# Five tiles of u instead of ten take their low parts through DRAM, and ten pairs instead of eleven in the first half of the down projection

## The chip, the cores and the metric

The kernel runs on one core of one Trainium2 chip. The core has a matrix engine (TensorE, PE in the profile), a vector engine (VectorE, DVE), an activation engine (ScalarE, ACT), GpSimd (POOL) and SyncE (SP); each works through its own list of instructions in order and waits at an instruction until what it needs is there. Transfers between DRAM and the on-chip memory are issued by ACT, POOL and SP, each from its own list, and run on 16 DMA engines that all three share. The metric is the device time of one execution in microseconds, smaller is better; the median of three runs is given.

## The reference

One decoder layer on x of 256 tokens by 2048 columns, in float32: a pre-norm, one input projection, two kinds of attention, an output projection with a post-norm, and then the feed-forward part, which is where the change is:

```
x   = x + RMSNorm_post(concat_heads(A, B) @ W_out)
x   = x + RMSNorm_post2(W_down relu(RMSNorm_pre2(x) @ W_up)^2)
```

W_up is 2048 x 8192 and W_down 8192 x 2048. Below, u stands for relu(...)^2, 256 x 8192, that is 16 tiles of 512 columns, u0 to u15.

## The kernel before

**Products.** Every float32 operand x is split into a high part and a low part: ACT writes `hi` (L311, or L315 with a gain), which rounds x to TensorE's fp32r type, and DVE writes `lo` = x - `hi` (L312, L316). A product is three matmuls: hi by hi, hi by lo, lo by hi (L301), each of 128 rows by 512 columns. Weights come tile by tile: SP loads 512 KB `raw` (five buffers), ACT and DVE split them into `hi` and `lo` (eight buffers each), up to six tiles ahead of TensorE. TensorE has no other work that it could turn to when a `lo` is late.

**Pairs.** Two such k tiles can be taken together as a "pair", in a scheme with seven instead of eight products of blocks (function `seven`): 21 instead of 24 matmuls for both. For that, 1 MB of weights is loaded by POOL into one of the buffers `ab`, `ab2`, `c`, `ab_down`, `u01` (L379), DVE makes two sums t and u of it (L366 to L371), four parts are split instead of two, and DVE makes sums on the activations' side too (q, then s; L1035 to L1037). DOWN_SEVEN lists which pairs kp are taken so in the two halves of the down projection. The s of pairs that both halves take (SHARED) are written to DRAM in the first half (L1029) and read back by POOL in the second.

**The up projection** runs in eight chunks of 1024 columns of W_up, from 360 to 710 us. A chunk j gives u tiles 2j and 2j+1. Chunks from 1 on have plain k tiles and three pairs. When a chunk ends, DVE adds its partial sums (L1101, L1163), and four times (two u tiles by two token blocks) a chain follows while the next chunk runs: ACT makes r, relu and square (L944, L945), into the ring `r` of three buffers, and writes it to DRAM as `rkeep` in 512-byte pieces (L947); after D_BACK it issues the read back (`turn_u`, L956), which has to wait until the write has landed, into a quarter of buffer `c`; DVE transposes this into the tile `uT` (L965). The detour does the part of the transpose that crosses groups of 32 partitions.

**Low parts of u.** For the tiles g in AWAY, `lo_away` puts u - hi(u) together in DRAM during the up projection: ACT writes -hi(u) in two halves, `neg`, into the same ring `r` (L979), and sends each to DRAM (L981, `ukeep<-neg`); after D_ADD, POOL issues for each half a transfer that adds u to what is there (L991, an accumulate). In the first half of the down projection POOL reads this back as `ulo` (L1021). For the other tiles, DVE makes `ulo` there itself (L312), and SP writes it to `ukeep` for the second half (`keep_u`, L1025).

**The down projection** has two halves c of 1024 output columns. Each goes through the 16 tiles of u in order, tile g holding k = 4g to 4g+3, which are the pairs kp = 2g and 2g+1. In the first half, pairs' weights come into `ab_down` and `c` by turns.

**The end.** `x_back` brings x back for the residual: the powers `pwn` that it was scaled with, in four small reads (L1216), then sixteen reads of 128 KB from `xkeep` (L1221), all on SP, and DVE scales them (L1227). `powers`, which writes `pwk` (L859), runs during the output projection, near 326 us.

**What sets the order.** The program is written out in one go by a planner: `Flow` keeps a clock that advances with each matmul by a modelled time, and chains that are due at a moment of it. `flow.start(gen, delay)` puts a chain in, `yield d` lets it sleep for d. Whenever the clock passes a chain's moment, its next instructions are written into the engines' lists. So a delay such as D_BACK doesn't make an engine wait; it decides behind which other instructions on its list a step stands. Where a step stands before its input is there, the engine waits, with all that is listed behind it.

Of the kernel before, what the change touches and what calls it, by code (L numbers as in the profile page):

```python
# [18 lines left out]
F32 = mybir.dt.float32  # L19
# [7 lines left out]
P = 128  # L27
D = 2048
S = 256
NB = S // P  # L30
# [15 lines left out]
CW = 1024  # L46
# [46 lines left out]

UP_STEP = 2.4

D_BACK, D_TURN, D_NEG, D_LO, D_ADD = 8.0, 8.0, 9.0, 2.0, 25.0


SUMS_AHEAD = 2
# [17 lines left out]
N_SEVEN = [sum(w == "w" for w, _ in steps) for steps in UP_STEPS]  # L117


DOWN_SEVEN = ((7, 9, 11, 13, 15, 19, 21, 23, 25, 27, 29), range(3, 28, 2))  # L120
AWAY = range(4, 14)
LATE = 10
SHARED = [k for k in DOWN_SEVEN[0] if k in DOWN_SEVEN[1]]
GT = FF // 512
# [144 lines left out]
def layer(nc, tc, io):  # L269
    flow = Flow()  # L270
# [78 lines left out]
    late = {}  # L349
# [97 lines left out]
    for c in range(2):  # L447
        wide_d.append([])
        for what, k in DOWN_STEPS[c]:
            if what == "k":  # L450
                ts = [weights.plan(down_weight(c, k), 1, CW)]
            else:
                q, parts_q, back = [lambda c=c, k=k, f=f: f(c, k) for f in (down_sums, down_split, down_back)]
# [232 lines left out]
    for half in range(2):  # L686
        qkv = {}
        for nms in (("qk", "v") if not half else "qkv"):
            accs = [acc for _, _, acc in proj(xT, [ch_a[half, nms]], f"{nms}{half}",
                                              bank_of=at_bank if (half, nms) == (0, "v") else None)]  # L690
            for i, nm in enumerate(nms):
                t = pa.tile([P, NB, 512], F32, tag=nm, name=f"{nm}_{half}")
# [149 lines left out]
    pwk, pwn = dram.tile([P, NB], F32, name="pwk"), con.tile([P, NB], F32, name="pwn")  # L842
    xkeep = [dram.tile([P, D], F32, name=f"xkeep{b}") for b in range(NB)]

    def powers():
        po, g_post = late["po"], late["g_post"]
        yield 8.0
        for n in range(4):
            junk = po.tile([P, 512], BF16, tag="junk", bufs=1, name=f"junkg{n}")
            nc.scalar.activation(junk, g_post[:, n * 512:(n + 1) * 512], AF.Square, accum_out=gg4[:, n:n + 1])  # L850
            yield 1.5
        nc.vector.reduce_sum(gg, gg4, axis=mybir.AxisListType.X)
        nc.vector.tensor_scalar_add(pws[:, 3, :], ss0, gg)
        r = rstd_of(pws[:, 3, :], NB, D, "pw")
        yield 2.0
        nc.vector.tensor_single_scalar(out=pw.bitcast(I32), in_=r.bitcast(I32), scalar=0x7F800000, op=OP.bitwise_and)
        nc.vector.tensor_single_scalar(out=pwi.bitcast(I32), in_=pw.bitcast(I32), scalar=0x7F800000, op=OP.bitwise_xor)
        nc.vector.tensor_scalar_mul(pwi, pwi, 0.5)
        nc.gpsimd.dma_start(out=pwk, in_=pwi)  # L859
        for i, (v, c) in enumerate(((pwi, 1.0 / D), (pwi, EPS), (pw, EPS))):  # L860
            nc.vector.scalar_tensor_tensor(out=pws[:, i, :], in0=v, scalar=c, in1=v, op0=OP.mult, op1=OP.mult)
        for b in range(NB):
            for c in (slice(0, CW), slice(CW, D)):
                nc.vector.tensor_scalar_mul(xs[b][:, c], xs[b][:, c], pw[:, b:b + 1])
                yield 1.5
# [74 lines left out]
    def up_evac(j, b, acc, order):  # L940

        yield UP_STEP * order
        r = late["up"].tile([P, 512], F32, tag="r", bufs=3, name=f"r{j}_{b}")
        nc.scalar.activation(r, acc, AF.Relu, scale=rstd2[b])  # L944
        nc.scalar.activation(r, r, AF.Square)  # L945
        keep = dram.tile([P, 512], F32, name=f"rkeep{j}_{b}")
        nc.scalar.dma_start(out=keep.rearrange("(a t) (q c) -> (t q) a c", a=4, q=4),  # L947
                            in_=r.rearrange("m (a c) -> m a c", a=4))
        flow.start(turn_u(j, b, keep), D_BACK)

    turned = set()

    def turn_u(j, b, keep):

        x = closing()[2 * b + j % 2]
        nc.scalar.dma_start(out=x, in_=keep)  # L956
        yield D_TURN
        if j not in uT:
            if j in (0, 1, 10, 11, 12, 13):
                t2 = late["u01" if j < 2 else "ab2" if j < 12 else "ab"][:, j % 2 * CW:(j % 2 + 1) * CW]  # L960
            else:
                tag = {"tag": "T", "bufs": 2} if j > 13 else {"tag": f"uT{j}", "bufs": 1}
                t2 = late["up"].tile([P, CW], F32, name=f"uT{j}", **tag)
            uT[j] = t2.rearrange("p (k s) -> p k s", k=4)
        nc.vector.transpose(uT[j][:, :, b * P:(b + 1) * P].rearrange("p k (q t) -> p k q t", q=4),  # L965
                            x.rearrange("p (q k c) -> p k q c", q=4, k=4))
        if b:
            turned.add(j)
            if j in AWAY:
                flow.start(lo_away(j), D_NEG)  # L970
# [133 lines left out]
    def closing():  # L1104
        return [late["c"][:, i * 512:(i + 1) * 512] for i in range(4)]
# [62 lines left out]
    up = late["up"]  # L1168
# [40 lines left out]

    def x_back():  # L1210

        def in_order(rows):
            return rows.rearrange("(t q) d -> q t d", q=4)

        for q in range(4):
            nc.sync.dma_start(out=pwn[32 * q:32 * q + 32], in_=in_order(pwk)[q])  # L1216
        for b in range(NB):
            for i in range(2):
                x = uT[6 + 2 * b + i].rearrange("p k s -> p (k s)")
                for q in range(4):  # L1220
                    nc.sync.dma_start(out=x[32 * q:32 * q + 32], in_=in_order(xkeep[b])[q, :, i * CW:(i + 1) * CW])  # L1221
                yield 2.0
        yield 20.0
        for b in range(NB):
            for i in range(2):
                x = uT[6 + 2 * b + i].rearrange("p k s -> p (k s)")
                nc.vector.tensor_scalar_mul(x, x, pwn[:, b:b + 1])  # L1227
                yield 1.5
# [152 lines left out]
```

## Time and profile before

| | us |
|---|---|
| median of 3 runs | 1062.83 (1059.89, 1062.83, 1066.42) |
| profiled execution | 1065.99 |
| its span | 1064.2, granted TensorE clock 0.990 on average |
| TensorE busy | 1038.5 |
| VectorE busy | 833.6 |
| ScalarE busy | 639.2 |
| GpSimd busy | 74.4 |

A span that TensorE fills to 98% has little waiting in it, and what there is lies in a few places; so the busy shares say only which engine is the bound. Where time is lost is read from windows of 10 us: the number of matmuls in one, and the granted clock. Who is to blame is read from the timeline of the engine that was late, where each row has the idle time before the instruction and what ended it. For a transfer the time from issue to landing counts, not that of its issue.

### The profile page before, as it was taken

To read this page: it belongs to the slowest core of one execution; us is meant where nothing else is said; L and a number is where in the kernel's file an instruction comes from. 1 tells how busy PE (TensorE), PEld (TensorE's weight loads), DVE (VectorE), ACT (ScalarE), POOL (GpSimd) and SP (SyncE) were. 2 spreads that over 40 slices of the span, in tenths; PEclk is the share of its full clock that TensorE was granted. 3 is DMA by queue.
4 is the path that set the end of the run, shared out by engine and by line. 5 is a ranking of instruction groups with operands and counts; after the bars stand their busy time and mean duration, and the time that the engine had idled before them with its cause. 6 is when DMAs were issued, how large, how long until landed. Compare 5 with 4: busy or idle time off the path is not lost.

```text
span 1064.2 us, 13304 instructions
## 1 busy us (share of the span) xinstructions
PE 1038.5 (98%) x4715; PEld 855.0 (80%) x4715; DVE 833.6 (78%) x1125; ACT 639.2 (60%) x862; POOL 74.4 (7%) x115
## 2 busy tenths in 40 slices
PE   9999999999999999999999999899799999999996
PEld 6888889888878788888888787687688888888875
DVE  6666536567556679999989789896699999999696
ACT  6674436565555457576666666675475665766571
POOL 0000000000000000000011110000210100111100
PEclk9999999999999999999999999999899999999999
DMA  9964447454447297777898898889979868888972
GB/s 310 359 216 144 139 126 241 141 159 158 139 173 223 80 379 256 245 247 243 288 278 263 249 288 266 245 291 307 283 256 390 276 222 309 283 329 296 323 263 79
DMA packets 108515, 259.74 MB, mean 244 GB/s; under 512 B 9120, under 2 KB 30112, under 8 KB 108064
## 3 DMA queue, kind: packets, MB, share of 16 engines
q1 hardware_dynamic: 64528, 169.90, 47.2%
q0 software_dynamic: 19104, 66.59, 19.8%
q10 hardware_dynamic: 24816, 22.40, 6.4%
q8 instruction: 37, 0.61, 0.2%
q14 instruction: 30, 0.25, 0.1%
HBM read 227.92 MB, written 30.93 MB: 243 GB/s over the span
## 4 chain that ended last, share of the span: by engine, by line
PE 71%; DMA 12%; DVE 7%; ACT 4%; issue 3%; ACTq 1%; POOL 0%; SPq 0%; DVEq 0%; POOLq 0%
PE y L301 19%; PE acc_u L301 12%; PE acc_o L301 8%; PE md L301 5%; PE acc_v L301 4%; PE acc_qk L301 4%; DMA ukeep<-neg 3%; DMA rkeep<-r 3%; DVE lo L312 2%; PE acc_ckv L301 2%; PE acc_q L301 2%; PE acc_k L301 2%; PE acc_cq L301 2%; PE acc_ukv L301 2%; PE m L301 2%
## 5 line engine op out<-in xcount | busy, mean ns | idle before, releaser
L312 DVE TENSOR_TENSOR lo<-raw,hi 128x1024 fp32r<-128x1024 f32 (+3 forms) x205 | 231.6, 1149 | 94.0 <-ACT hi L311 93.0
L311 ACT ACTIVATE hi<-raw 128x1024 fp32r<-128x1024 f32 (+3 forms) x205 | 201.2, 995 | 71.9 <-DMA raw<-in_w_in 16.7
L301 PE MATMUL acc_u<-lo,hT_hi 128*128 128x512 f32 x386 | 151.8, 393 | 6.3 <-DVE lo L316 6.3
L301 PE MATMUL acc_u<-hi,hT_hi 128*128 128x512 f32 x386 | 152.1, 394 | 0.0
L301 PE MATMUL acc_u<-hi,hT_lo 128*128 128x512 f32 x386 | 151.6, 393 | 0.4 <-DVE hT_lo L312 0.4
L301 PE MATMUL y<-lo,uhi 128*128 128x512 f32 x352 | 139.0, 395 | 6.5 <-DVE lo L312 6.5
L301 PE MATMUL y<-hi,uhi 128*128 128x512 f32 x352 | 138.3, 393 | 1.9 <-ACT uhi L311 1.9
L301 PE MATMUL y<-hi,ulo 128*128 128x512 f32 x352 | 138.5, 394 | 0.5 <-DVE ulo L312 0.5
L315 ACT ACTIVATE hi<-raw,gcol 128x1024 fp32r<-128x1024 f32 x86 | 97.2, 1148 | 39.3 <-DMA raw<-in_w_up 20.0
L316 DVE SCALAR_TENSOR_TENSOR lo<-raw,gcol,hi 128x1024 fp32r<-128x1024 f32 x86 | 107.2, 1276 | 11.1 <-ACT hi L315 11.0
L301 PEld LDWEIGHTS acc_u<-lo,hT_hi 128*128 128x128 f32 x386 | 73.3, 190 | 22.7 <-DVE lo L316 7.5
L301 PEld LDWEIGHTS acc_u<-hi,hT_lo 128*128 128x128 f32 x386 | 73.2, 190 | 16.3 <-DVE hT_lo L312 0.8
L301 PEld LDWEIGHTS acc_u<-hi,hT_hi 128*128 128x128 f32 x386 | 73.0, 189 | 15.3 <-ACT hi L315 0.2
L301 PEld LDWEIGHTS y<-lo,uhi 128*128 128x128 f32 x352 | 66.9, 190 | 21.4 <-DVE lo L312 7.3
L301 PEld LDWEIGHTS y<-hi,uhi 128*128 128x128 f32 x352 | 66.8, 190 | 16.6 <-ACT uhi L311 2.3
L301 PEld LDWEIGHTS y<-hi,ulo 128*128 128x128 f32 x352 | 66.9, 190 | 15.0 <-DVE ulo L312 1.0
L312 DVE TENSOR_TENSOR lo<-st_down,hi 128x1024 fp32r<-128x1024 f32 x48 | 57.5, 1220 | 0.7 <-ACT hi L311 0.7
L311 ACT ACTIVATE hi<-st_down 128x1024 fp32r<-128x1024 f32 x48 | 49.9, 1052 | 4.9 <-DVE st_down L371 3.9
L301 PE MATMUL acc_o<-hi,mixT_hi 128*128 128x512 f32 x128 | 52.4, 410 | 0.0
L301 PE MATMUL md<-hi,s 128*128 128x512 f32 x144 | 52.1, 389 | 0.0
L301 PE MATMUL acc_o<-hi,mixT_lo 128*128 128x512 f32 x128 | 50.7, 396 | 0.0
L301 PE MATMUL acc_o<-lo,mixT_hi 128*128 128x512 f32 x128 | 50.5, 395 | 0.0
(332 smaller groups left out, 2032.1 us busy)
## 6 DMA issues: line engine op xcount, KB each, us to landing
raw<-in_w_up SPq DMA_DIRECT2D x86, 512.0 KB, 4.9
raw<-in_w_down SPq DMA_DIRECT2D x80, 512.0 KB, 6.6
raw<-in_w_in SPq DMA_DIRECT2D x55, 512.0 KB, 5.0
ab<-in_w_up POOLq DMA_DIRECT2D x17, 1024.0 KB, 6.8
raw<-in_w_out SPq DMA_DIRECT2D x32, 512.0 KB, 4.1
ab_down<-in_w_down POOLq DMA_DIRECT2D x13, 1024.0 KB, 9.8
ulo<-ukeep POOLq DMA_DIRECT2D x25, 512.0 KB, 6.7
rkeep<-r ACTq DMA_DIRECT2D x32, 256.0 KB, 3.6
```

What stands on the lines that cost most here:

```text
L301: nc.tensor.matmul(out, a, b, start=start, stop=stop)
L311: nc.scalar.activation(hi, src, AF.Copy)
L312: nc.vector.tensor_tensor(out=lo, in0=src, in1=hi.bitcast(F32), op=OP.subtract)
L315: nc.scalar.activation(hi, src, AF.Copy, scale=g)
L316: nc.vector.scalar_tensor_tensor(out=lo, in0=src, scalar=g, in1=hi.bitcast(F32), op0=OP.mult, op1=OP.subtract)
```

## The change

Five things are edited.

1. DOWN_SEVEN loses pair kp 7 in the first half (eleven pairs become ten); its two k tiles are done plainly there. The second half still has it and so makes its own s.
2. AWAY becomes 5, 7, 9, 11, 13. For u4, u6, u8, u10 and u12 DVE makes `ulo` in the first half, and SP writes it out.
3. D_BACK goes from 8 to 12 (20 for the last of the last chunk), D_ADD from 25 to 26. The planner thus writes the reads of `rkeep` and the accumulates at other places.
4. The x tiles of u14 and u15, which are read back at the start of the down projection, lie in ring `r` and no longer in `c`.
5. `pwn` is read by POOL in `powers`, not by SP in `x_back`, and the sixteen reads of `xkeep` are written 1.6 apart in the planner's clock, with a pause of 6 instead of 20 behind them.

```diff
--- before.py
+++ after.py
@@ -93,7 +93,7 @@
 
 UP_STEP = 2.4
 
-D_BACK, D_TURN, D_NEG, D_LO, D_ADD = 8.0, 8.0, 9.0, 2.0, 25.0
+D_BACK, D_TURN, D_NEG, D_LO, D_ADD = 12.0, 8.0, 9.0, 2.0, 26.0
 
 
 SUMS_AHEAD = 2
@@ -117,8 +117,8 @@
 N_SEVEN = [sum(w == "w" for w, _ in steps) for steps in UP_STEPS]
 
 
-DOWN_SEVEN = ((7, 9, 11, 13, 15, 19, 21, 23, 25, 27, 29), range(3, 28, 2))
-AWAY = range(4, 14)
+DOWN_SEVEN = ((9, 11, 13, 15, 19, 21, 23, 25, 27, 29), range(3, 28, 2))
+AWAY = range(5, 14, 2)
 LATE = 10
 SHARED = [k for k in DOWN_SEVEN[0] if k in DOWN_SEVEN[1]]
 GT = FF // 512
@@ -842,6 +842,9 @@
     pwk, pwn = dram.tile([P, NB], F32, name="pwk"), con.tile([P, NB], F32, name="pwn")
     xkeep = [dram.tile([P, D], F32, name=f"xkeep{b}") for b in range(NB)]
 
+    def by_quarter(rows):
+        return rows.rearrange("(t q) d -> q t d", q=4)
+
     def powers():
         po, g_post = late["po"], late["g_post"]
         yield 8.0
@@ -859,6 +862,8 @@
         nc.gpsimd.dma_start(out=pwk, in_=pwi)
         for i, (v, c) in enumerate(((pwi, 1.0 / D), (pwi, EPS), (pw, EPS))):
             nc.vector.scalar_tensor_tensor(out=pws[:, i, :], in0=v, scalar=c, in1=v, op0=OP.mult, op1=OP.mult)
+        for q in range(4):
+            nc.gpsimd.dma_start(out=pwn[32 * q:32 * q + 32], in_=by_quarter(pwk)[q])
         for b in range(NB):
             for c in (slice(0, CW), slice(CW, D)):
                 nc.vector.tensor_scalar_mul(xs[b][:, c], xs[b][:, c], pw[:, b:b + 1])
@@ -946,13 +951,17 @@
         keep = dram.tile([P, 512], F32, name=f"rkeep{j}_{b}")
         nc.scalar.dma_start(out=keep.rearrange("(a t) (q c) -> (t q) a c", a=4, q=4),
                             in_=r.rearrange("m (a c) -> m a c", a=4))
-        flow.start(turn_u(j, b, keep), D_BACK)
+        flow.start(turn_u(j, b, keep), D_BACK + (8.0 if (j, b) == (GT - 1, NB - 1) else 0.0))
 
     turned = set()
 
     def turn_u(j, b, keep):
 
-        x = closing()[2 * b + j % 2]
+        o = 2 * b + j % 2
+        if j < GT - 2:
+            x = closing()[o]
+        else:
+            x = late["up"].tile([P, 512], F32, tag="r", bufs=3, name=f"x{j}_{b}")
         nc.scalar.dma_start(out=x, in_=keep)
         yield D_TURN
         if j not in uT:
@@ -1209,18 +1218,13 @@
 
     def x_back():
 
-        def in_order(rows):
-            return rows.rearrange("(t q) d -> q t d", q=4)
-
-        for q in range(4):
-            nc.sync.dma_start(out=pwn[32 * q:32 * q + 32], in_=in_order(pwk)[q])
         for b in range(NB):
             for i in range(2):
                 x = uT[6 + 2 * b + i].rearrange("p k s -> p (k s)")
                 for q in range(4):
-                    nc.sync.dma_start(out=x[32 * q:32 * q + 32], in_=in_order(xkeep[b])[q, :, i * CW:(i + 1) * CW])
-                yield 2.0
-        yield 20.0
+                    nc.sync.dma_start(out=x[32 * q:32 * q + 32], in_=by_quarter(xkeep[b])[q, :, i * CW:(i + 1) * CW])
+                    yield 1.6
+        yield 6.0
         for b in range(NB):
             for i in range(2):
                 x = uT[6 + 2 * b + i].rearrange("p k s -> p (k s)")
```

What the planner makes of it is seen in the engines' lists. First the end of up chunk 4, on ACT: `neg6_0`, `neg7_1` are halves of the negs of u6 and u7, `r8_0` is the r of u8 for token block 0. Before:

```order
L315 ACTIVATE hi229_5111<-raw229_5109,gcol_69 128x1024
L981 DMA ukeep6_5063<-neg6_1_5106 128x512
L979 ACTIVATE neg7_1_5128<-uT7_4965 128x512
L311 ACTIVATE hi230_5138<-ab_3505 128x512
L981 DMA ukeep7_5097<-neg7_1_5128 128x512
L944 ACTIVATE r8_0_5155<-acc_u4_00_4760,rstd_pre20_3347 128x512
L945 ACTIVATE r8_0_5155<-r8_0_5155 128x512
L947 DMA rkeep8_0_5158<-r8_0_5155 128x4x128
L311 ACTIVATE hi231_5165<-ab_3505 128x1024
L944 ACTIVATE r9_0_5178<-acc_u4_01_4761,rstd_pre20_3347 128x512
L945 ACTIVATE r9_0_5178<-r9_0_5178 128x512
L947 DMA rkeep9_0_5181<-r9_0_5178 128x4x128
```

After (the lines of this part of the code are numbered 5 to 9 higher):

```order
L988 ACTIVATE neg7_0_5113<-uT7_4992 128x512
L311 ACTIVATE hi230_5123<-ab_3509 128x512
L990 DMA ukeep7_5112<-neg7_0_5113 128x512
L949 ACTIVATE r8_0_5140<-acc_u4_00_4754,rstd_pre20_3351 128x512
L950 ACTIVATE r8_0_5140<-r8_0_5140 128x512
L952 DMA rkeep8_0_5143<-r8_0_5140 128x4x128
L311 ACTIVATE hi231_5150<-ab_3509 128x1024
L988 ACTIVATE neg7_1_5160<-uT7_4992 128x512
L949 ACTIVATE r9_0_5165<-acc_u4_01_4755,rstd_pre20_3351 128x512
L950 ACTIVATE r9_0_5165<-r9_0_5165 128x512
L952 DMA rkeep9_0_5168<-r9_0_5165 128x4x128
L990 DMA ukeep7_5112<-neg7_1_5160 128x512
```

Of four halves of negs two are left, and the second now stands behind the first r, with its write behind the second.

The start of up chunk 5, on ACT: reads of `rkeep` into `c`, between the `hi` of weights. Before:

```order
L315 ACTIVATE hi234_5236<-raw234_5234,gcol_69 128x1024
L956 DMA c_3507<-rkeep8_0_5158 128x512
L956 DMA c_3507<-rkeep9_0_5181 128x512
L315 ACTIVATE hi235_5260<-raw235_5258,gcol_69 128x1024
L311 ACTIVATE hi236_5264<-ab2_3506 128x512
L311 ACTIVATE hi237_5271<-ab2_3506 128x1024
L311 ACTIVATE hi238_5281<-u5_1_5230 128x1024
L956 DMA c_3507<-rkeep8_1_5202 128x512
L311 ACTIVATE hi239_5292<-t5_1_5229 128x1024
L315 ACTIVATE hi240_5310<-raw240_5308,gcol_69 128x1024
L956 DMA c_3507<-rkeep9_1_5223 128x512
```

After:

```order
L315 ACTIVATE hi234_5224<-raw234_5222,gcol_69 128x1024
L315 ACTIVATE hi235_5246<-raw235_5244,gcol_69 128x1024
L311 ACTIVATE hi236_5250<-ab2_3510 128x512
L311 ACTIVATE hi237_5257<-ab2_3510 128x1024
L965 DMA c_3511<-rkeep8_0_5143 128x512
L311 ACTIVATE hi238_5268<-u5_1_5218 128x1024
L311 ACTIVATE hi239_5278<-t5_1_5217 128x1024
L965 DMA c_3511<-rkeep9_0_5168 128x512
L315 ACTIVATE hi240_5297<-raw240_5295,gcol_69 128x1024
L965 DMA c_3511<-rkeep8_1_5190 128x512
L311 ACTIVATE hi241_5314<-ab_3509 128x512
L965 DMA c_3511<-rkeep9_1_5211 128x512
```

The first read has moved behind the fourth `hi` of this stretch, the last from behind the seventh to behind the eighth.

POOL's list across chunks 3 to 5, where `ukeep6 <- uT6` is an accumulate of u6. Before:

```order
L379 DMA ab2_3506<-in_w_up 128x2x1024
L379 DMA ab_3505<-in_w_up 128x2x1024
L991 DMA ukeep6_5063<-uT6_4950 128x512 x2
L991 DMA ukeep7_5097<-uT7_4965 128x512 x2
L379 DMA ab2_3506<-in_w_up 128x2x1024
L379 DMA ab_3505<-in_w_up 128x2x1024
L991 DMA ukeep8_5437<-uT8_5324 128x512 x2
L991 DMA ukeep9_5471<-uT9_5339 128x512 x2
```

After:

```order
L379 DMA ab2_3510<-in_w_up 128x2x1024
L379 DMA ab_3509<-in_w_up 128x2x1024
L1000 DMA ukeep7_5112<-uT7_4992 128x512
L379 DMA ab2_3510<-in_w_up 128x2x1024
L1000 DMA ukeep7_5112<-uT7_4992 128x512
L379 DMA ab_3509<-in_w_up 128x2x1024
L1000 DMA ukeep9_5477<-uT9_5357 128x512
L379 DMA ab_3509<-in_w_up 128x2x1024
L1000 DMA ukeep9_5477<-uT9_5357 128x512
```

Four accumulates between two loads of weights have become one at a time, between each two loads.

## The prediction

> **What bounds the kernel now.** First the page's busy shares, then the waits of TensorE (PE) from 590 us on (columns: total us, times, longest), then windows of 10 us (stretch, length, then busy us and count for PE, PEld, DVE, ACT and POOL, then granted clock, DMA share and GB/s).
>
> ```profile
> PE 1038.5 (98%) x4715; PEld 855.0 (80%) x4715; DVE 833.6 (78%) x1125; ACT 639.2 (60%) x862; POOL 74.4 (7%) x115
> PE y L301 <- DVE lo L312: 6.5, 2, 5.3
> PE acc_u L301 <- DVE lo L316: 6.3, 3, 3.4
> PE y L301 <- ACT uhi L311: 1.9, 1, 1.9
> 600.00:610.00 10.00, 7.49 (x25) 5.35 (x24) 9.37 (x11) 7.47 (x9) 0.74 (x1) 0.83 0.57 213
> 610.00:620.00 10.00, 10.00 (x46) 8.19 (x45) 9.79 (x11) 6.50 (x9) 0.91 (x1) 1.00 0.95 285
> 630.00:640.00 10.00, 9.23 (x41) 7.29 (x40) 6.82 (x8) 8.54 (x12) 0.85 (x1) 1.00 0.93 212
> 680.00:690.00 10.00, 6.55 (x23) 4.91 (x22) 9.70 (x11) 5.78 (x7) 0.00 (x0) 0.83 0.69 206
> 730.00:740.00 10.00, 7.60 (x25) 5.51 (x24) 7.57 (x8) 8.63 (x11) 0.00 (x0) 0.83 0.97 311
> 750.00:760.00 10.00, 7.63 (x34) 6.00 (x32) 1.40 (x2) 2.34 (x4) 4.36 (x6) 0.99 0.93 273
> 760.00:770.00 10.00, 7.02 (x23) 5.68 (x24) 9.83 (x14) 4.95 (x6) 0.72 (x1) 0.67 1.04 334
> 1010.00:1020.00 10.00, 8.84 (x39) 6.92 (x38) 9.86 (x11) 7.48 (x9) 1.58 (x3) 1.00 1.02 404
> ```
>
> PE is the bound: it is busy 98% of the span. An undisturbed stretch (610:620) holds 46 matmuls, so one costs 10/46 = 0.217 us. Each other row is short of 46, and the shortfall times 0.217 us prices a stall, clock included: 600:610 loses 4.6, 630:640 1.1, 680:690 5.0, 730:740 4.6, 750:770 7.6 and 1010:1020 about 1.2 (its idle time; some records can be missing). I round these to 4.5, 1.0, 5.0, 4.5, 7.5 and 1.2, together 23.7 us; they are called stalls 1 to 6. Where the clock column says 0.83, the half rate lasted 10 x 0.17/0.5 = 3.4 us and cost 1.7 us on top of the waiting. Windows with little idle time (0.77 in 630:640, 1.16 in 1010:1020) kept 1.00.
>
> [...]
>
> Next, who is late. The chain of waits (start, us, what) and ACT's own timeline (idle time before and its releaser in brackets):
>
> ```profile
> 585.09 13.99 DMA rkeep<-r
> 661.28 7.68 DMA ukeep<-neg
> 719.19 12.90 DMA rkeep<-r
> 599.47 1.06 ACT L311 ACTIVATE hi<-t 128x1024 fp32r<-128x1024 f32 x1 [5.74 <-DMA rkeep<-r]
> 604.11 1.58 ACT L311 ACTIVATE hi<-ab 128x512 fp32r<-128x512 f32 x2 [2.53 <-DMA rkeep<-r]
> 669.05 0.69 ACT L944 ACTIVATE r<-acc_u,rstd_pre 128x512 f32<-128x512 f32 x1 [3.59 <-DMA ukeep<-neg]
> 728.71 0.69 ACT L944 ACTIVATE r<-acc_u,rstd_pre 128x512 f32<-128x512 f32 x1 [5.14 <-DMA rkeep<-r]
> ```
>
> Stall 1: ACT writes r to DRAM (`rkeep`) and some 8 us later issues the read back (L956); the write took 14 us, so ACT stood twice with its `hi` work queued behind the read, 5.74 + 2.53 us. Stalls 2 and 3: an `r` needs one of three ring buffers, and a `neg` still sits there until its write lands (7.68 us). Stall 4: the fourth r waits 5.14 us for the first r's write. Stall 5 is another thing:
>
> ```profile
> 748.10 0.70 DVE L965 STREAM_TRANSPOSE uT<-c 128x512 f32<-128x512 f32 x1
> 749.10 0.73 POOL L379 DMA_DIRECT2D c<-in_w_down  x1 [36.30 <-DMA ukeep<-ulo]
> 759.11 1.23 DVE L366 TENSOR_TENSOR st_down<-c 128x1024 f32<-128x1024 f32 x1 [8.60 <-DMA c<-in_w_down]
> 1009.68 1.22 DVE L366 TENSOR_TENSOR st_down<-u 128x1024 f32<-128x1024 f32 x1 [5.06 <-DMA u<-in_w_down]
> L1221 SPq DMA_DIRECT2D uT<-xkeep x16: 302/355/569, 978.8 to 996.0; - x16
> ```
>
> The 1 MB load into `c` goes out only when the last transpose of u15 has read `c` (748.10 + 0.70), although the bracket names a `ukeep` write; DVE then waits 8.60 us for it. Stall 6: in 978.8 to 996.0 sixteen reads of `xkeep` go out, and the pair into `u` is 5.06 us late.
>
> **The change part by part.**
>
> (1) The x tiles of u14 and u15 move out of `c`. The transposes no longer hold the load back; it follows the adds of chunk 7 and, in POOL's queue, one half accumulate of u13 that waits for its neg. Even at 730 it leads its old start by 19 us, and the first pair (kp 9) now comes from `ab_down`, `c` serving kp 11. Stall 5 goes: -7.5. The x tiles now take the `r` ring, where they wait for writes of the same burst; u15 is first used 15 tiles later, so I price that at 0.
>
> (2) Reads 12 instead of 8 after the r, and half as many negs and accumulates. The landing times (min/median/max) of four groups: `rkeep` writes in a boundary without accumulates (489:500), those of stall 1 (585:588), the accumulates issued with them (583:587), and all twenty writes of negs.
>
> ```profile
> DMA to landing us min/median/max: 2.3/3.4/5.5
> DMA to landing us min/median/max: 14.0/14.9/15.8
> DMA to landing us min/median/max: 9.3/11.0/13.9
> DMA to landing us min/median/max: 2.6/6.3/8.4
> ```
>
> In stall 1 the r's shared the DMA with 1 MB of `ab` and four accumulates; afterwards one accumulate is left there, so the write lies between 3.4 and 14.9. I take 6 to 8, nearer the quiet row, since three of four accumulates are gone. The read back, 4 us later, then finds it landed. Even at 14 the wait falls from 5.74 to about 2. Stall 1: 4.5 to 0 (0 to 2). In stall 2 two negs are left of four: 1.0 to 0 (0 to 2).
>
> The ring now runs neg_0, r0, neg_1, r1, r2, r3 at five boundaries: r1 waits for neg_0's write, r2 for r0's, r3 for neg_1's. Between the write of neg_1 and r3 lie about two `hi` (1.06 us each) and r2 in two steps of 0.69, with the issues 4 us; the same for r0 and r2. What lands within 4 us costs nothing; what lands later delays the two or three `hi` behind. How much of that PE bears shows a `lo` pair in a quiet chunk, with the matmul that first uses it:
>
> ```profile
> 502.30 2.47 DVE L316 SCALAR_TENSOR_TENSOR lo<-raw,gcol,hi 128x1024 fp32r<-128x1024 f32 x2
> 508.94 0.39 PE L301 MATMUL acc_u<-lo,hT_hi 128*128 128x512 f32 x1
> ```
>
> The first of the two ends at 503.5 and is used 5.4 us later: the room at its tightest there. Stall 3: r0 stands in a boundary without accumulates ahead of it (3.4 us), neg_1 takes 2.6 to 8.4, so r3 waits 0 to 4 and the room takes it. 5.0 becomes 1 (0 to 5). Stall 4: `ab_down` and two accumulates stay beside the r's, so I keep 12.90 us for their writes; r2, not r3, then waits some 9 us, r3 perhaps for neg_1 as well, and the reads of x come later than before, off ACT's path. 4.5 becomes 4 (0 to 8).
>
> Five tiles fewer also take ten neg writes, ten accumulates and five `ulo` reads out, and add five 512 KB writes on SP (L1025), each waiting for DVE's `ulo` with the next raw load behind it; raw tiles run up to six ahead, so 0 (0 to 1).
>
> (3) DVE makes five more `ulo`, and pair kp 7 becomes two plain tiles. The rows: a stretch of the first half with its DVE count, DVE's groups in 711:881, and `lo` of the tile that is used tightest, with its matmul.
>
> ```profile
> 833.00:874.00 41.00, 41.00 (x182) 33.95 (x181) 40.49 (x49) 27.82 (x33) 3.22 (x5) 1.00 0.72 246
> L312 DVE TENSOR_TENSOR lo<-raw,hi 128x1024 fp32r<-128x1024 f32 x40 | 47.5, 1219 | 9.8 <-ACT hi L311 9.8
> L312 DVE TENSOR_TENSOR ulo<-uT,uhi 128x1024 fp32r<-128x1024 f32 x4 | 4.8, 1210 | 0.7 <-ACT uhi L311 0.7
> L370 DVE TENSOR_TENSOR st_down<-st_down,ab_down 128x512 f32<-128x512 f32 x6 | 4.2, 692 | 0.2
> L312 DVE TENSOR_TENSOR s<-st_down,s 128x512 fp32r<-128x512 f32 x11 | 7.5, 681 | 0.8 <-ACT s L311 0.8
> L1035 DVE TENSOR_TENSOR st_down<-uT 128x256 f32<-128x256 f32 x7 | 2.9, 413 | 0.0
> 864.05 1.22 DVE L312 TENSOR_TENSOR lo<-raw,hi 128x1024 fp32r<-128x1024 f32 x1
> 867.49 0.39 PE L301 MATMUL y<-lo,uhi 128*128 128x512 f32 x1
> ```
>
> Five `ulo` cost 5 x 1.21 = 6.05 us. A pair costs DVE 1.22 (t, as at 1009.68) + 2 x 0.69 (u), 0.68 + 3 x 1.22 (four low parts, the b11 one like s) and 0.41 + 2 x 0.3 + 0.68 (q, s), together 8.6 (0.3 is estimated for the two 128-wide sums from the 256-wide 0.41); two plain tiles cost 2.44. So -6.2: the sum is even, but the place isn't. From kp 19 on pairs and plain tiles alternate; in 833:874 DVE is busy 40.49 of 41 us, and the `lo` that ends at 865.27 is wanted at 867.49: a room of 2.2 us. `ulo` of u10 and u12 take 2.4 of it. I put 1 us of PE waiting here (0 to 4: all five `ulo`, less the 2.2). What is saved at kp 7 and the 18 plain tiles at the start give the first alternating stretch more room.
>
> (4) PE: 24 instead of 21 matmuls at kp 7, 3 x 0.217 = +0.65. In the second half kp 7 makes s again (1.65 us on DVE, no read); 0, since plain tiles kp 0 to 2 lie ahead of it.
>
> (5) `pwn` is read on POOL right after `pwk`, and the sixteen `xkeep` reads are spaced 1.6 apart:
>
> ```profile
> 325.73 0.81 POOL L859 DMA_DIRECT2D pwk<-pwi  x1 [1.38 <-DVE pwi L858]
> 353.94 0.57 POOL L506 TENSOR_TENSOR rstd_post<-t_post,neg_half 128x1 f32<-128x1 f32 x1 [27.40 <-DVE t_post L505]
> ```
>
> POOL had nothing between 326.5 and 353.94, so its wait for `pwk` is hidden. Stall 6: 1.2 to 0.3 (0 to 1.2).
>
> Sum: -4.5 - 1.0 - 4.0 - 0.5 - 7.5 - 0.9 + 1.0 + 0.65 = -16.8. The profiled execution took 1065.99 us (span 1064.2 and 1.8 around it), 3.2 above the median of 1062.83. 1065.99 - 16.8 = 1049.2; from the median it would be 1046.0. A run that is faster already may have less of these stalls to lose, so I go between the two, nearer the upper: **1048**.
>
> **The rivals.**
> (a) The waits at stalls 3 and 4 and half of stall 1 stay, because a neg stands between the r's. For: the negs took up to 8.4 us, and three buffers remain. Against: half as many. Then only 5, 6, 2 and half of 1 go: 7.5 + 0.9 + 1.0 + 2.2 - 1.65 = 10, and 1053 to 1056.
> (b) The r writes stay near 14 us although accumulates go, since any work of POOL's queue beside them slows their small pieces: stall 1 stays, and 1048 + 4.5 = 1052.5. Against: 3.4 in the quiet boundary. [...] The rows of 3.4 and 14.9 don't separate number from presence.
> (c) DVE becomes the bound of the first half: all five `ulo` late, 6.05 us, and two half-rate spells of 1.7, less the 1 counted: 8.5, so 1056. Against: the 18 plain tiles at the start.
> (d) Slower: the neg between the r's lands as late as the late r's of stall 1, 14 us instead of 6.3. r3 then waits 14 - 4 = 10 at the four boundaries before the last; 5.4 is covered, and PE loses 4.6 + 1.7 each, 25 us, less the 1 kept for stall 3: 1072, slower than before. It decides from a landing of about 12 us: (12 - 9.4 + 1.7) x 4 = 17 eats the whole sum. Against: no neg took over 8.4.
> (e) The change doesn't thin the bursts: an accumulate of u7 still goes out at the r's of stall 1, and the rest only moves. Then stalls 1 to 4 stay, and (1) and (5) leave 8.4 - 1.65 = 6.8: 1056 to 1059.
>
> **How the numbers follow.** The forecast has 0.52, on 1041 to 1053: from the median with stall 4 gone too (1046 - 4, and the last tenths of 6), up to 1049.2 with stall 4 at its bound of 8. Then (a) 0.15, (b) 0.10, (c) 0.10, (d) 0.07, (e) 0.06. 1% of 1062.83, about what separates a change from none here, is 10.6: faster is below 1052.2, slower above 1073.5. Faster: nearly all of the forecast, half of (b), some of (a) and (c) from the lower end of the runs, 0.62. Slower: over half of (d), 0.05. Same: the rest, 0.33. The range, 1041 to 1058, holds the forecast, (a), (b) and (c), and leaves out (d), part of (e) and the tails.
>
> **What would show it.** Right: no DVE wait on `c<-in_w_down` near 759; no ACT wait on `rkeep` near 599; clock 1.00 in 600:610 and 750:770; `rkeep` at 3 to 8 us in the boundary with the accumulate of u7; DVE's wait for `u` near 1009 gone. Wrong: ACT's r waiting for `ukeep<-neg` over 5 us at the boundaries, PE waiting for DVE's `lo` or `ulo` in kp 21 to 29, `rkeep` still at 14 us near 590.

## The result, and the profile after

| | before | after |
|---|---|---|
| median of 4 runs | 1061.36 us | 1050.17 us (1047.15 to 1053.54) |
| ratio | | 0.9878, 95% interval 0.984 to 0.9915 |
| profiled execution | 1065.99 us | 1050.24 us |
| its span, mean granted clock | 1064.2 us, 0.990 | 1048.5 us, 0.995 |

The change makes the kernel 1.2% faster: 11.2 us by the medians, 15.75 us between the two profiled executions, of which the one before was among its slower runs. The stalls keep their numbers. First the busy shares of the changed kernel:

```profile
PE 1035.0 (99%) x4718; PEld 853.5 (81%) x4718; DVE 834.7 (80%) x1125; ACT 634.7 (61%) x850; POOL 64.1 (6%) x102
```

TensorE's waits for other engines in the down projection (total us, times, longest):

```profile
PE y L301 <- ACT uhi L311: 2.3, 1, 2.3
PE y L301 <- DVE ulo L312: 0.6, 2, 0.4
PE y L301 <- DVE lo L312: 0.4, 1, 0.4
```

Windows of 10 us, with the columns of before; the work behind stall 3 runs some 8 us earlier now, so that stall 4 is found in 720:730:

```profile
600.00:610.00 10.00, 10.00 (x45) 8.19 (x44) 9.90 (x12) 7.94 (x8) 0.00 (x0) 1.00 0.89 289
630.00:640.00 10.00, 10.00 (x45) 8.20 (x45) 9.97 (x12) 5.61 (x7) 1.62 (x2) 1.00 0.94 314
680.00:690.00 10.00, 10.00 (x45) 8.22 (x44) 9.58 (x12) 7.67 (x8) 0.00 (x0) 1.00 0.83 286
720.00:730.00 10.00, 7.47 (x19) 5.09 (x19) 8.19 (x10) 8.32 (x10) 0.00 (x0) 0.66 0.86 295
750.00:760.00 10.00, 10.00 (x46) 8.29 (x45) 6.23 (x9) 4.30 (x6) 2.01 (x3) 1.00 0.98 270
760.00:770.00 10.00, 10.00 (x46) 8.29 (x45) 9.64 (x11) 6.00 (x7) 0.56 (x1) 1.00 0.71 258
```

Stalls 1, 2, 3 and 5 are gone: these windows are full, at clock 1.00. Of stall 6 is left 0.4 us (the wait for `lo`). TensorE's two waits for `ulo` are 0.2 us at stall 4 and 0.4 near 852. Stall 4 is there still, and longer: 2.53 us idle and (1 - 0.66) x 10 = 3.4 us lost to the half rate (the granted clock is 0.50 from 723.2 to 730.0), 5.9 us (27 matmuls short of 46, at 0.217 us, say the same), where 4.6 were lost before. With 0.4 us near 852 and the 0.4 of stall 6 it is all that TensorE still waits between 590 us and the end of its work.

How it comes about is seen in the timelines of ACT, POOL and DVE of the changed kernel:

```profile
716.33 0.69 ACT L949 ACTIVATE r<-acc_u,rstd_pre 128x512 f32<-128x512 f32 x1 [7.40 <-DMA rkeep<-r]
699.45 0.73 POOL L379 DMA_DIRECT2D ab_down<-in_w_down  x1 [32.98 <-PE acc_u L301]
705.24 0.87 POOL L1000 DMA_DIRECT2D ukeep<-ab  x1 [5.06 <-DMA ukeep<-neg]
705.81 1.03 POOL L379 DMA_DIRECT2D c<-in_w_down  x1
747.00 1.23 DVE L366 TENSOR_TENSOR st_down<-c 128x1024 f32<-128x1024 f32 x1
```

The landing times (min/median/max) of the first two r writes there (701:707), and of two late r writes in the boundary of stall 1 (580:585):

```profile
DMA to landing us min/median/max: 12.3/13.0/13.6
DMA to landing us min/median/max: 5.9/6.9/8.0
```

The third r stands 7.40 us for the write of the first, which takes 13.6 us. Beside it run 1 MB into `ab_down` and, new in this place, 1 MB into `c`, whose load left at 705.81 instead of 749.10; DVE uses it at 747.00, without a wait. Of the half accumulates of u13 one (705.24) goes out in this burst. At stall 1 the writes take 5.9 to 8.0 us where they took 14.0 to 15.8 in the profiled execution before.

DVE's wait for the pair into `u`, late in the second half, is 1.5 instead of 5.06 us:

```profile
DVE st_down L366 <- DMA u<-in_w_down: 1.5, 1, 1.5
```

### The profile page after: what moved, and what is told of

Same layout as the page of the kernel before. It is cut to its first block, busy times and chain, and to the rows that moved or that the text cites. A ratio compares the mean times of both kernels' runs of the same rounds, so it can differ in the third digit from the quotient of the medians.

```text
span 1048.5 us, 13268 instructions
## 1 busy us (share of the span) xinstructions
PE 1035.0 (99%) x4718; PEld 853.5 (81%) x4718; DVE 834.7 (80%) x1125; ACT 634.7 (61%) x850; POOL 64.1 (6%) x102
## 4 chain that ended last, share of the span: by engine, by line
PE 76%; DVE 10%; issue 6%; DMA 5%; ACT 2%; POOL 1%; ACTq 0%; DVEq 0%; POOLq 0%; SPq 0%
PE acc_u L301 22%; PE y L301 13%; PE acc_o L301 8%; PE m L301 5%; PE acc_qk L301 4%; DVE lo L312 4%; PE acc_v L301 4%; PE md L301 3%; PE acc_ckv L301 2%; PE acc_q L301 2%; PE acc_k L301 2%; PE acc_cq L301 2%; PE acc_ukv L301 2%; PE acc_uq L301 2%; DMA ab_down<-in_w_down 1%
## 5 line engine op out<-in xcount | busy, mean ns | idle before, releaser
L312 DVE TENSOR_TENSOR lo<-raw,hi 128x1024 fp32r<-128x1024 f32 (+3 forms) x207 | 234.0, 1150 | 95.2 <-ACT hi L311 94.4
L311 ACT ACTIVATE hi<-raw 128x1024 fp32r<-128x1024 f32 (+3 forms) x207 | 203.3, 996 | 72.6 <-DMA raw<-in_w_down 15.9
L301 PE MATMUL y<-hi,uhi 128*128 128x512 f32 x358 | 140.7, 393 | 2.3 <-ACT uhi L311 2.3
L301 PE MATMUL y<-hi,ulo 128*128 128x512 f32 x358 | 140.8, 393 | 0.6 <-DVE ulo L312 0.6
L312 DVE TENSOR_TENSOR lo<-st_down,hi 128x1024 fp32r<-128x1024 f32 x46 | 55.1, 1221 | 0.8 <-ACT hi L311 0.8
L311 ACT ACTIVATE hi<-u 128x1024 fp32r<-128x1024 f32 (+1 forms) x33 | 32.4, 982 | 29.5 <-PE y L301 12.3
```

Source lines behind the costliest of these rows:

```text
L301: nc.tensor.matmul(out, a, b, start=start, stop=stop)
L311: nc.scalar.activation(hi, src, AF.Copy)
L312: nc.vector.tensor_tensor(out=lo, in0=src, in1=hi.bitcast(F32), op=OP.subtract)
```

## The experiments

The times, each against runs of the kernel before on the same chip:

| run | edit | median us | ratio, 95% interval |
|---|---|---|---|
| e1_x_alone | before + edit 4 | 1057.56 | 0.9954 (0.9937 to 0.9971) |
| e2_delays_alone | before + edit 3 | 1076.93 | 1.0133 (1.0098 to 1.0167) |
| e3_away_alone | before + edit 2 | 1057.67 | 0.9949 (0.9932 to 0.9966) |
| e4_ten_alone | before + edit 1 | 1055.45 | 0.9927 (0.9905 to 0.9948) |
| e5_x_undone | after - edit 4 | 1051.5 | 0.9887 (0.9863 to 0.991) |
| e6_eleven | after - edit 1 | 1054.6 | 0.9927 (0.9906 to 0.9949) |
| e7_delays_undone | after - edit 3 (but the last chunk) | 1051.26 | 0.9895 (0.9864 to 0.9926) |
| e9_away_undone | after - edit 2 | 1069.34 | 1.006 (1.0036 to 1.0085) |
| e8_xback_undone | after - edit 5 | 1047.27 (one run) | |
| e10_no_away | after, no tile in AWAY | 1049.54 | 0.9862 (0.9825 to 0.9899) |
| i1_c_after_neg | after, `c` load later | 1051.03 | 0.9883 (0.9857 to 0.9909) |
| i1b_both_after_neg | after, both loads later | 1045.94 | 0.9835 (0.981 to 0.986) |

### One edit alone

**The delays** (e2_delays_alone).

```diff
-D_BACK, D_TURN, D_NEG, D_LO, D_ADD = 8.0, 8.0, 9.0, 2.0, 25.0
+D_BACK, D_TURN, D_NEG, D_LO, D_ADD = 12.0, 8.0, 9.0, 2.0, 26.0
```

> The kernel before with edit 3 alone (D_BACK 12, D_ADD 26). If a read 4 us later is enough: the r writes of stall 1 still take 10 to 15 us beside three accumulates, ACT waits under 2.5 us for them instead of 5.74, and TensorE's stop near 605 goes (-4.5). If it takes fewer accumulates: the stop stays above 2 us. In both, the transposes of u15 come 4 us later, so the load into c does too, and stall 5 grows from 7.5 to about 11: the time comes out within 3 us of before.

It was 1.3% slower, where at most 3 us had been expected. ACT's waits between 400 and 760 us, and TensorE's at stall 4:

```profile
ACT r L944 <- DMA rkeep<-r: 17.6, 5, 7.6
ACT r L944 <- DMA ukeep<-neg: 12.5, 4, 4.6
PE y L301 <- ACT uhi L311: 7.7, 1, 7.7
```

The landing of two r writes beside `ab` and three accumulates (538:542):

```profile
DMA to landing us min/median/max: 8.6/9.0/9.5
```

The window of stall 4:

```profile
740.00:750.00 10.00, 3.60 (x8) 2.39 (x9) 7.79 (x10) 8.94 (x12) 0.00 (x0) 0.67 0.82 271
```

ACT no longer waits at the reads of x, as expected: no `hi` waits for an r write any more. But the chain that makes the negs starts when a tile has been turned, so it moved 4 us too, and now the last of the four halves of negs stands behind the first r instead of ahead of it, in a ring of three. The r's wait 30.1 us for the ring (20.6 before). Stall 4 became 7.7 us with two spells of half rate. Neither expectation had that: the edit hurts at the boundaries, while stall 5, which was to grow to 11, took 4.3 us and one spell.

**Five tiles** (e3_away_alone).

```diff
-AWAY = range(4, 14)
+AWAY = range(5, 14, 2)
```

> The kernel before with edit 2 alone (AWAY 5, 7, 9, 11, 13; reads still 8 behind). My theory: one or two accumulates beside the r's of stall 1, their writes at 6 to 10 us instead of 14 to 16, no ACT wait above 3 us near 599; stalls 1, 2 and 3 go (-8 to -10), 4, 5 and 6 stay; DVE makes five more ulo with all eleven pairs kept, which costs 0 to 4 us between kp 9 and 29: near 1054. Rival (DVE is the bound there): PE waits for DVE's lo or ulo 4 to 8 us in all, and no gain is left.

TensorE's and DVE's waits in the down projection:

```profile
PE y L301 <- DVE lo L312: 7.9, 3, 6.6
DVE st_down L366 <- DMA c<-in_w_down: 8.2, 1, 8.2
```

Stalls 1 to 3 are gone without any other edit: TensorE has no stop over 0.1 us between 400 and 720. Stall 5 stays, 6.6 us with two spells of half rate. TensorE waits for `ulo` 1.4 us in three places, 0.5 of it at stall 4 and 0.3 behind stall 5, so that at most the other 0.5, and 0.4 of waiting for `lo` near 786, falls to DVE's five more, with all eleven pairs. It gained 5.4 us (0.0051 x 1062) where I expected 8. In part stall 5 took more than before: 740:760 is 41 matmuls short of 92, 8.9 us against 7.6.

**Ten pairs** (e4_ten_alone).

```diff
-DOWN_SEVEN = ((7, 9, 11, ...
+DOWN_SEVEN = ((9, 11, ...
```

> The kernel before with edit 1 alone (ten pairs; x of u14 and u15 still in c). The first pair is kp 9 and takes ab_down; c serves kp 11, about 12 us later than it served kp 9. If that is enough, stall 5 goes here too, without the x tiles being moved (-7.5 + 0.65, near 1055); if the load into c still comes too late, DVE waits 2 to 5 us for it and half of stall 5 stays (1058). Stalls 1 to 4 and 6 stay.

DVE's and TensorE's waits, and then two windows, that of stall 1 and one near the end:

```profile
DVE st_down L366 <- DMA c<-in_w_down: 5.9, 2, 3.2
PE acc_u L301 <- DVE lo L316: 4.7, 2, 3.0
```

```profile
600.00:610.00 10.00, 10.00 (x45) 7.96 (x44) 9.93 (x12) 7.30 (x8) 0.74 (x1) 1.00 0.78 260
1000.00:1010.00 10.00, 8.21 (x30) 6.27 (x29) 8.99 (x10) 7.55 (x9) 1.58 (x3) 0.83 1.03 421
```

DVE waits 3.2 us at the longest for `c`, and TensorE doesn't stop: stall 5 goes by the order of the pairs alone. Stalls 2 and 3 (the second row) and 4 stay; 6 (the second window) took 1.8 us and a spell of half rate. Stall 1, which was to stay, is not there (the first window), although nothing was changed for it: from 555 to 612 us ACT and POOL have the same instructions in the same order as before, and ACT's wait near 597 is still 4.53 us, where it was 5.74:

```profile
597.42 1.06 ACT L311 ACTIVATE hi<-t 128x1024 fp32r<-128x1024 f32 x1 [4.53 <-DMA rkeep<-r]
```

**The x tiles** (e1_x_alone). The ring needs the later reads in the last chunk, so these came along for that chunk.

```diff
-        flow.start(turn_u(j, b, keep), D_BACK)
+        flow.start(turn_u(j, b, keep), (D_BACK if j < GT - 2 else 12.0) + (8.0 if (j, b) == (GT - 1, NB - 1) else 0.0))
...
-        x = closing()[2 * b + j % 2]
+        o = 2 * b + j % 2
+        if j < GT - 2:
+            x = closing()[o]
+        else:
+            x = late["up"].tile([P, 512], F32, tag="r", bufs=3, name=f"x{j}_{b}")
```

> The kernel before with edit 4 alone (x of u14 and u15 in the ring r, their reads 12 and 20 behind). My theory: the load into c leaves near 712 instead of 749 and DVE's wait of 8.60 us for it goes (stall 5, -7.5 us); stalls 1, 2, 3 and 6 stay. The load now runs beside the r writes of the last chunk, which stay at 13 us or rise, so stall 4 stays at 4.5 to 8: in sum 4 to 8 us faster, near 1055. Rival (the x tiles in the ring hold the r's up): TensorE's stop near 734 grows by as much as stall 5 shrinks, no gain.

ACT's wait in the last boundary, TensorE's behind it, and the window of stall 1:

```profile
ACT r L944 <- DMA rkeep<-r: 7.0, 1, 7.0
PE y L301 <- ACT uhi L311: 2.7, 1, 2.7
```

```profile
600.00:610.00 10.00, 9.27 (x41) 7.27 (x40) 9.93 (x12) 8.62 (x10) 0.74 (x1) 1.00 0.70 236
```

No wait for `c` is left, and stall 4 takes 2.7 + 0.7 us and a spell of half rate: 720:740 is 27 matmuls short of 92, 5.9 us in all against 4.6, the first r write taking 15.0 us. The gain is 4.9 us (0.0046 x 1062). Stall 1 took 0.7 us here and kept full clock, with ACT's list unchanged there. Edits 1 and 4 thus each remove stall 5.

### One edit undone

**Ten tiles again** (e9_away_undone).

```diff
-AWAY = range(5, 14, 2)
+AWAY = range(4, 14)
```

> The changed kernel with edit 2 undone (ten tiles put their low parts together in DRAM). By the run of the delays alone, where r's waited 17.6 us for r writes and 12.5 us for negs: four halves of negs stand between the r's at D_BACK 12, the ring is full at each boundary, ACT waits 15 to 30 us for it in all, PE stops near 550, 595, 640 and 690, and stall 4 is longer than in the changed kernel; edits 1 and 4 keep stall 5 away. 1060 to 1072, that is 10 to 20 us slower than the changed kernel. If the delays hurt only through the late load into c (the rival), it is within 3 us of it.

ACT's waits between 400 and 760 us, and TensorE's from 400 on:

```profile
ACT r L949 <- DMA ukeep<-neg: 16.6, 5, 4.0
ACT r L949 <- DMA rkeep<-r: 14.1, 5, 5.0
PE acc_u L301 <- DVE lo L316: 7.4, 4, 3.4
PE y L301 <- ACT uhi L311: 4.8, 1, 4.8
```

Slower than before the change, by 0.6%, and 19 us slower than the changed kernel: the r's wait 30.7 us for the ring, and TensorE stops near 552, 595, 640 and 690. So the later delays of edit 3 need edit 2. What edits 1, 4 and 5 gain together without these two was not run; alone, 1 and 4 each gained (e4, e1).

**The delays of before** (e7_delays_undone).

```diff
-D_BACK, D_TURN, D_NEG, D_LO, D_ADD = 12.0, 8.0, 9.0, 2.0, 26.0
+D_BACK, D_TURN, D_NEG, D_LO, D_ADD = 8.0, 8.0, 9.0, 2.0, 25.0
```

> The changed kernel with the delays of before for chunks 0 to 6 (D_BACK 8, D_ADD 25; the last chunk keeps 12 and 20, which the ring needs). If the five tiles alone took stalls 1 to 3 away, as the run of edit 2 alone says, the time is that of the changed kernel within 2 us, TensorE has no stop between 590 and 700, and stall 4 is as it is there. If the delays are needed too, a stop of 1 us or more shows near 600, 640 or 685, and it is 3 to 8 us slower than the changed kernel.

The same time as the changed kernel, no stop between 400 and 720, and stall 4 much as there (2.3 and 0.7 us and one spell of half rate; the first r write took 16.0 us). With five tiles the delays do nothing for stalls 1 to 3.

**x back in c** (e5_x_undone).

```diff
-        o = 2 * b + j % 2
-        if j < GT - 2:
-            x = closing()[o]
-        else:
-            x = late["up"].tile([P, 512], F32, tag="r", bufs=3, name=f"x{j}_{b}")
+        x = closing()[2 * b + j % 2]
```

> The changed kernel with edit 4 undone (x of u14 and u15 back in c, reads still 12 and 20 behind). My theory of stall 4: the load into c, free to leave at 705.8 since edit 4, slows the r writes (13.6 us) and so makes the third r wait 7.40 us. Here it leaves only after the last transpose of u15, near 745; the wait of the r falls to 4 to 5 us, as in the two kernels where c also leaves late (4.5 and 4.4), and TensorE's stop near 723 is below 1 us. In exchange the sums of kp 11 (747.0) wait 5 to 9 us for c, and PE stops for 0 to 4 us near 755. The time is within 3 us of the changed kernel. Rival (c has nothing to do with the r writes): the stop near 723 stays at 2.3 us with half clock.

DVE's waits for `c`, then the window in which TensorE stops for it:

```profile
DVE st_down L366 <- DMA c<-in_w_down: 8.3, 2, 8.0
```

```profile
750.00:760.00 10.00, 7.83 (x35) 6.18 (x34) 6.08 (x7) 2.64 (x3) 0.00 (x0) 1.00 0.87 308
```

As expected: 2.17 us of stop near 757 in place of stall 4, whose rest is 0.6 + 0.7 us at full clock; the time is the same. But that rest is not the late `c` alone: the first neg of u13 took 9.4 us here and 5.0 in the changed kernel, so the second r waited 4.2 us for its buffer, and the third, coming later, no longer waited for the first r's write, which took 11.8 us.

**Eleven pairs again** (e6_eleven).

```diff
-DOWN_SEVEN = ((9, 11, ...
+DOWN_SEVEN = ((7, 9, 11, ...
```

> The changed kernel with edit 1 undone (pair kp 7 back, eleven pairs). TensorE does 0.65 us less. DVE does 6.2 us more ahead of kp 9, and five ulo more than the kernel before in all. If the room holds: the time is within 2 us of the changed kernel, PE waits for DVE's lo or ulo less than 2 us between 740 and 870. If DVE is the bound there (rival c): PE waits 3 to 6 us, with half-rate spells, and it is 4 to 9 us slower than the changed kernel. The first pair's sums come some 5 us earlier, so a wait for ab_down near 729 can show.

The load into `c`, the landing of the first r write of the last boundary (702.9), then TensorE's waits from 400 us on:

```profile
703.66 0.74 POOL L379 DMA_DIRECT2D c<-in_w_down  x1 [2.26 <-ACT r L950]
```

```profile
DMA to landing us min/median/max: 17.6/17.6/17.6
```

```profile
PE y L301 <- ACT uhi L311: 6.1, 1, 6.1
PE y L301 <- DVE ulo L312: 0.2, 1, 0.2
```

4 us slower than the changed kernel, but not by DVE: TensorE waits 0.2 us for `lo` and 0.2 for `ulo` between 725 and 870. It is stall 4 that has grown to 6.1 us. With eleven pairs the load into `c` is listed ahead of the half accumulate of u13 and leaves at 703.7, beside the first r write. So edit 1 is worth its 4 us by where it puts a transfer (the intervals of the two kernels just overlap), and rival (c) is out.

**x_back** (e8_xback_undone).

```diff
...
-                    yield 1.6
-        yield 6.0
+                yield 2.0
+        yield 20.0
```

(and `pwn` is read there again, by SP.)

> The changed kernel with edit 5 undone (pwn and sixteen xkeep reads of SP in one run, as before). Stall 6 comes back: DVE waits 4 to 6 us for the pair into u near 993 and PE 1.0 to 1.8 us, against 0.39 in the changed kernel; the time is 0 to 2 us more, below what one look can tell. If the reads are not the cause, PE's stop there stays below 0.7.

DVE's wait for the pair into `u` (940 to 1030) and TensorE's behind it, then the load into `c` and the landing of the first r write in the last boundary (703.3):

```profile
DVE st_down L366 <- DMA u<-in_w_down: 5.1, 2, 4.7
PE y L301 <- DVE lo L312: 1.0, 1, 1.0
```

```profile
710.94 1.04 POOL L379 DMA_DIRECT2D c<-in_w_down  x1
```

```profile
DMA to landing us min/median/max: 11.3/11.3/11.3
```

Stall 6 is back: 4.7 and 1.0 us against 1.5 and 0.4. That the one run is faster than the changed kernel's median comes from another place. In the last boundary ACT's writes and `hi` and POOL's transfers have the same order in both kernels, but here the neg that the accumulate waits for took 9.1 us instead of 5.0, the load into `c` behind it left at 710.9 instead of 705.8, the first r write took 11.3 us, and TensorE stopped for 0.7 us instead of 2.5 with half rate. So stall 4 can come out one way or the other with the same order; why the neg landed later stays open. The changed kernel's own runs, 1047.15 to 1053.54, lie about as far apart; whether it is by this, their times alone don't say.

### No tile away

(e10_no_away)

```diff
-AWAY = range(5, 14, 2)
+AWAY = ()
```

> The changed kernel with no tile at all in AWAY: no negs, no accumulates, DVE makes all sixteen ulo in the first half (five more than after the change, +6.05 us of DVE). The r ring holds r's alone, so only the third wait of the last chunk stays: r writes beside both 1 MB loads, fourth r waits 3 to 8 us, stall 4 0 to 5 us. In the first half the pairs alternate with plain tiles and every tile now costs DVE 1.21 more: each cycle of two pairs and two plain tiles loses 0.9 + 2.4 us of room, six such cycles, so PE waits 3 to 8 us for DVE (rival c made real): 1050 to 1058. If the room is larger than I read, PE waits under 2 us and it is no slower than the changed kernel.

TensorE's waits from 400 us on, then a window of 20 us of the first half:

```profile
PE y L301 <- DVE ulo L312: 2.0, 3, 0.7
PE y L301 <- DVE lo L312: 1.2, 4, 0.4
```

```profile
831.00:851.00 20.00, 18.61 (x79) 14.37 (x77) 19.66 (x25) 14.04 (x17) 1.43 (x2) 1.00 0.75 255
```

Five more `ulo`, 6.05 us of DVE, cost TensorE 2.0 us in short stops at full clock between 838 and 852, where the changed kernel lost 0.4; stall 4 shrank to 0.9 us. The time is that of the changed kernel: the detour of the low parts through DRAM buys nothing measurable here, with ten pairs and the other edits in place.

### What ends stall 4

**The load into c later** (i1_c_after_neg); both accumulates of u13 stand behind `ab_down` and ahead of `c` in POOL's list, and the second waits for the second neg.

```diff
-            yield 4.0 + 5.0 * (g % 2) + 20.0 * ((g - LATE) // 2)
+            yield 4.0 + 5.0 * (g % 2) + (20.0 if g == 13 else 0.0)
...
-            yield 2.0 if g < LATE else 10.0
+            yield 2.0 if g < LATE else 1.0 if g == 13 else 10.0
```

> The changed kernel with one thing moved: the second half accumulate of u13 stands ahead of the load into c in POOL's list, so that this load waits until the second neg of u13 has landed (about 715 instead of 705.8). By my theory of stall 4 the r writes take 8 to 11 us, the third r waits 3 to 5 us instead of 7.40, uhi of tile 2 comes 3 us earlier and the stop near 723 with its half clock goes: 4 to 6 us faster than the changed kernel, near 1045. c still lands by 730, 15 us ahead of its use. If the load of ab_down is the cause and not c: the wait stays at 7 us and so does the time.

The landing of the first r write in the last boundary, then ACT's wait at a read of x:

```profile
DMA to landing us min/median/max: 10.9/10.9/10.9
```

```profile
ACT hi L311 <- DMA rkeep<-r: 8.6, 1, 8.6
```

The third r waits 0.9 us and the stop near 721 is 0.1 + 0.7 us at full clock, but `c`, leaving at 717.8, now runs beside the last r write (13.5 us); ACT waits 8.6 us at its read, and TensorE stops 1.3 us twice, near 735. The wait moved, and the time is the same.

**Both loads later** (i1b_both_after_neg): the first line with 0.0 in place of 20.0, which puts the accumulates ahead of `ab_down` too.

> As the run before, but both accumulates of u13 stand ahead of the load into ab_down as well, so that both 1 MB loads leave only when the second neg of u13 has landed. By my theory the first r writes land in 3 to 6 us, no r waits over 2 us, stall 4 goes (-5 to -6 us against the changed kernel). Price: the late r writes and the reads of x run beside 2 MB of loads; if that makes ACT wait over 5 us at a read, or ab_down misses the sums of kp 9 near 734, half of the gain comes back as a stop between 725 and 745.

The first two r writes, the window of stall 4, and all that TensorE waits for other engines between 400 and 1030 us:

```profile
DMA to landing us min/median/max: 4.6/6.1/7.7
```

```profile
720.00:730.00 10.00, 10.00 (x46) 8.29 (x45) 9.32 (x12) 6.41 (x8) 0.92 (x2) 1.00 1.06 322
```

```profile
PE y L301 <- DVE lo L312: 0.6, 1, 0.6
PE y L301 <- DVE ulo L312: 0.2, 1, 0.2
```

Stall 4 is gone. The two loads take 15.2 and 19.5 us now; DVE waits 1.9 us for `ab_down` and 4.2 for a raw tile there, and TensorE waits for no other engine between 700 and 760. 1045.94 us: this beats the kernel before, and each of its runs (1044.71 to 1047.23) is below each run of the three other kernels measured beside it (e5, e7, i1: from 1049.08 up). Its median is 4 us below that of the changed kernel too, but against that one the two intervals just overlap, and the two were not run side by side.

## Why the prediction was right, and where it wasn't

The forecast was 1048 us, the result 1050.17, inside 1041 to 1058. The sum against the profiled run was -16.8, and -15.75 was measured.

- **Stall 1**, "4.5 to 0": right, and by the step given: the late r writes took 5.9 to 8.0 us, forecast 6 to 8, nearer the quiet row. But the prediction gave the gain to two edits, the later reads and the fewer accumulates, and only the second did it (e3, e7). "Even at 14 the wait falls from 5.74 to about 2" holds for the reads, and left out that the same delay moves a neg between the r's; with ten tiles that costs more than it saves (e2, e9). The 1.7 us of half rate went with the gap (600:610 at clock 1.00). What was not sound is the price of 4.5: it came from one execution, and with the same order on ACT and POOL the stall took 0.7 us in e1 and none in e4, where ACT's longest wait was 4.45 and 4.53 us instead of 5.74. So ACT's wait is what edit 2 removed, and how much of 4.5 us that is worth by the median is not shown.
- **Stalls 2 and 3**, "0" and "1": both 0. r3 did not wait for neg_1 before the last boundary.
- **Stall 4**, "4 (0 to 8)": 5.9. The mechanism was right (r2 waits for r0's write: "some 9", measured 7.40). The term that was mis-sized is what this wait costs: 4 for a wait of 9, while 7.40 cost a stop of 2.3 us and, behind it, two spells of half rate (3.4 us), which the 4 did not name. And that r0's write took 13.6 us, near the 12.90 of step (2), is luck in part. That step had two accumulates beside the r's, where one is left; and step (1) counted the earlier load into `c` as a gain only, while its 1 MB landed in this very burst. r0's write took 17.6 and 16.0 us with `c` leaving 0.7 to 0.8 us behind it (e6, e7), 13.6 with 3.2 us (the changed kernel), 10.9 to 11.8 with 7.6 us or more (e8, e5, i1), and 4.6 with neither load (i1b). So the loads set how late r0's write lands; in e5, e6, e8 and i1, where the first neg of u13 took 8.9 to 9.4 us, the second r waited for that as well.
- **Stall 5**, "-7.5": right. The prediction named both that `c` is free earlier and that it serves a later pair, and booked it under edit 4. Either is enough: alone, the two were worth 4.9 (e1) and 7.8 us (e4, 0.0073 x 1062 by the ratio), and with edit 4 undone the changed kernel is no slower (e5), with 2.2 us of stop for `c` left. These are differences of whole runs, not of stall 5 alone.
- **Stall 6**, "0.3": 0.4. **TensorE**, "+0.65": the three matmuls are there (4718 instead of 4715).
- **DVE**, "1 (0 to 4)": 0.6 with part of it at stall 4. The even sum of 6.05 and 6.2 was right, and the room was larger than I priced: without kp 7's relief TensorE waited 0.4 us for DVE between 725 and 870 (e6), with five more `ulo` 2.0 us (e10).
- **The step from the profiled run to the median** was the weak one: 1065.99 was at the high end of the runs before, and I carried 14.8 of the 16.8 us over to the median. By medians it was 11.2. Stall 1, which e1 and e4 show small or absent with the same order, is one part of that.

Of the rivals, (a) holds for stall 4 alone. (b), that any work of POOL's queue holds the r's up as much as four accumulates, is refuted: beside `ab` the late r writes took 5.9 to 8.0 us with one accumulate, 7.3 to 8.8 with two (e3), 8.6 to 9.5 with three (e2), and with four 14.0 to 15.8 before, 11.5 to 14.7 in e1 and e4. The more was queued, the later the writes landed; how the queues share the DMA engines, no run shows. (c) is out. (d) was right in kind for another kernel than the one I priced: with ten tiles the ring does make it slower than before (e9), yet with negs landing in 3.0 to 10.2 us at the four boundaries before the last, below the 12 us that I had as its threshold: negs and r's both fill the ring, and the r's waits add up to 30.7 us.

## What to carry to other kernels

A load that is set free early starts early; look at what it then runs beside, and hold it until just before it is needed if short transfers with someone waiting are in the way (`c`, leaving at 705.8 instead of 749.1, and `ab_down` ran beside a first r write of 13.6 us; with neither beside it the write took 4.6, i1b). A ring of buffers that are freed by a transfer's landing makes every other user of the ring a possible wait (30.1 us of the r's waiting in e2, 20.6 before), so a change of delay that seems to concern one step has to be read off the whole list of the engine. And of edits that were made together, several may remove the same stall (edits 1 and 4 each removed stall 5): undo each one alone before crediting it. A stall that was read off one execution can be absent from the next with the same lists (stall 1: 4.6 us before, none in e4); look at a second one before pricing it.

## What the runs showed of the hardware

The half rate of TensorE did not follow from the length of a stop alone. In e4_ten_alone a window with 1.79 us idle (1000:1010, clock 0.83) brought a spell of it; in e5_x_undone one with 2.17 us (750:760, clock 1.00) did not. The spell was 3.4 us long there (10 x 0.17/0.5) and in the kernel before (606.2 to 609.6 at clock 0.50). It was 6.8 us, counted as two spells, in 720:730 of the changed kernel (10 x 0.34/0.5; a matmul started every 0.43 us, and every 0.23 ahead of the stop), after a stop of 2.3 us and, already at half rate, one of 0.2. What decides whether a stop brings a spell, these runs don't show.

A write of 256 KB in 512-byte pieces landed in 2.3 to 5.5 us with no accumulate beside it (489:500 before, DMA share 0.66) and in 17.6 us beside two loads of 1 MB and an accumulate (e6); with the same order of transfers, a 256 KB write of a neg took 5.0 us in one execution (the changed kernel) and 9.1 in another (e8).
